# Dilated attention in a hybrid block: V as weights on column halves, unsplit fp32 scores, shares spread by TensorE, y_b products between the attention groups

## The chip, the core and the metric

The kernel runs on one core of one Trainium2 chip. TensorE multiplies, VectorE (DVE), ScalarE (ACT) and GpSimd (POOL) work on tiles, and SyncE (SP) issues most of the DMAs. The metric is device microseconds of one execution; less is better.

## The reference, cut to what matters

One decoder block on x of [1, 2048, 1024], all fp32. The part that the change touches:

```python
proj = x @ w_in + b_in            # q, k, v for 3 groups of 8 heads of 64, gates, RG-LRU input
q, k = rope(q), rope(k)
for g, (window, dilation) in enumerate(((128, 1), (512, 4), (2048, 16))):
    # per residue of the dilation, blocks of 128 queries against the block before and their own
    s = einsum(q, k) * 64 ** -0.5          # masked to a band
    m = max(s); p = exp(s - m); l = sum(p)
    o[g] = einsum(p, v) / l
    lse[g] = m + log(l)
attn = sum_g softmax_g(lse) * o[g]         # weighted over the three groups
y_a = (attn * silu(g_attn)) @ w_attn_proj
h = rg_lru(causal_conv(u))                 # the second branch
y_b = (h * silu(g_lru)) @ w_lru_proj
merged = sigmoid(gA) * y_a + sigmoid(gB) * y_b
x = layer_norm(ALPHA * x + merged @ w_out + b_out)
```

With dilation 16 a residue has 128 positions, one block, so there is no block before it.

## The kernel before

Large products run in fp32r: each fp32 operand is split into a high part and a rest, and three products (high by high, high by rest, rest by high) replace one. The order of work on every engine is that of the program text: the kernel schedules by hand, with `later(lag, fn)` putting a step off by some ticks and `run(late)` issuing what is due. All engines take their instructions in that order, each from its own queue.

There are four stages.

1. *Projection* (`product`, `evacuate`, the chains): x @ w_in in a seven-product block scheme, with rotary q and k stored to `qk_scr`, v to `v_scr`, gates to `ga_scr` and `mg_scr`, and the RG-LRU's result to `hb_scr`.
2. *Attention*, in 12 units (`unit(u)`): four pairs of heads `hp`, and for each the dilations 1, 16, 4 in this order. A unit has 16 query blocks of 128, taken in pairs `j` (96 in all).
   - `k_split` and `q_split` bring q and k of the next unit into high and rest, on ScalarE and GpSimd.
   - `scores(j)`: two blocks by two heads, three fp32r products each, into the PSUM tiles s0 and s1 (one per head, [128, 2, 256], two buffers each). The heads use the lower and upper 64 rows of TensorE.
   - `weigh(m)`: for each head VectorE adds the mask and takes the minimum of the negated scores (the negated maximum) in one operation (L1016); ScalarE takes the exponential (L1018). p is [query, key].
   - `turn_p(j)`: TensorE transposes p in 64-row halves into t0 and t1 (L1032); `copy_p(j, e)` copies them to SBUF, half on ScalarE (L1045), half mostly on VectorE (L1047).
   - `values(j)` (L1063): the turned p, 128x128, is the weight, and 65 columns of V move (64 and a column of ones, which gives the sum l), per block, head and key block. The result o is [query, head column] in a PSUM tile with two buffers. VectorE copies it to `osb` (L1068), and GpSimd's queue sends it with the minima to `o_scr`.
   - Two pairs j make a group of work on TensorE: transposes, scores, scores, transposes, values, values; values lag the scores by two to three pairs.
3. *y_b and combination*: 32 jobs `yb_job(n)`, n = (column chunk c, output tile f), of 24 matmuls of 128x512 (L1299 to L1301), each followed by VectorE's product with the gate. Between them run 16 `combine(c, hp)`: three `oc` tiles are loaded from `o_scr`, VectorE and ScalarE work out the shares of the three dilations, GpSimd weights and adds, TensorE turns the sum back to [head column, position] (L1235), VectorE multiplies by the gate, and the result goes to `at_scr`.
4. *y_a and output*: `ya_job` (L1374 to L1376) on tiles from `at_scr`, and `out_job` (L1411 to L1413), with the layer norm.

The y_b jobs start when the last value products have been issued, because their pools open there. PSUM has eight banks of 2 KB a partition; in the attention s0 and s1 take four, t0 and t1 two, o two.

The lines that a wait on o and s depends on:

```python
bank = [aps.tile([P, 2, 256], F32, tag=f"s{h}", name=f"s{h}{j}", bufs=2) for h in range(2)]
...
o = aps.tile([P, 2, 130], F32, tag="o", name=f"o{j}", bufs=2)
...
dve.tensor_copy(osb[:, b:b + 2, 0:130], o)
```

Of the kernel before, what the change touches and what calls it, by code (L numbers as in the profile page):

```python
# [15 lines left out]
P = 128  # L16
# [15 lines left out]
def hybrid_block_kernel(ctx: ExitStack, tc: tile.TileContext, a: dict, out: bass.AP):  # L32
# [10 lines left out]
    o_scr = [[dram.tile([S, 132], F32, name=f"o_scr{g}{hp}") for hp in range(HP)] for g in range(3)]  # L43
# [28 lines left out]
    bn = cst.tile([P, 72], F32, name="bn")  # L72
    lr = cst.tile([P, 8, 8], F32, name="lr")
# [23 lines left out]
    X = ctx.enter_context(tc.tile_pool(name="X", bufs=1))  # L97

    def big(slot, shape, dt, name):
        return (Y if slot[0] == "Y" else Z if slot[0] == "Z" else X).tile(shape, dt, name=name, tag=slot)  # L100

# [40 lines left out]
    LAST_SLOTS = [*range(15, 19), *range(29, 32), *range(28, 18, -1), *range(14, -1, -1)]  # L142
# [254 lines left out]
    def silu_chain(y, sgn, f, c):  # L397
# [3 lines left out]
        act.activation(y, y, AF.Identity, scale=0.5 * sgn, bias=bh[:, f:f + 1])  # L401
# [370 lines left out]
    QSLOT, KSLOT = ("X3", "X1", "Y0"), ("X4", "Y3")  # L772
    VSLOT = {(0, 0): "X5", (2, 0): "Y1", (1, 0): "Y2", (0, 1): "X5", (2, 1): "Y1", (1, 1): "Y2"}
    KR = {}

    units = {}
# [5 lines left out]
    def k_parts(u):  # L782

        g, hp = unit(u)
        src = qk_scr["k", 4 * g + hp].rearrange("(d h) s -> h d s", h=2)

        def part(h, hs):
            def fn():
                if h == 0 and u % 2 == 0:
                    KR["t"] = big(("X2", "X0")[u // 2 % 2], [P, 2, S], F32R, f"C{u}")  # L790
                if h == 0:
                    units[u] = [None, None, KR["t"][:, u % 2]]
                sp.dma_start(flat(units[u][2][hs]), src[h])
            return fn

        return [part(0, lo_), part(1, up_)]

    def k_split(u, x):

        if x == 0:  # L800
            units[u][1] = big(KSLOT[u % 2], [P, S], F32R, f"B{u}")

        def piece(t):
            if unit(u)[0] == 2:
                return t.rearrange("p (c x) -> p c x", c=4)[:, :, 256 * x:256 * x + 256]
            return t[:, 1024 * x:1024 * x + 1024]

        lo, hi = piece(units[u][2]), piece(units[u][1])
        pool.tensor_copy(hi, flat(lo))
        pool.tensor_tensor(out=lo, in0=flat(lo), in1=flat(hi), op=ALU.subtract)  # L810

    def q_parts(u):

        g, hp = unit(u)
        q = qk_scr["q", 4 * g + hp].rearrange("(d h) s -> h d s", h=2)

        def part(h):
            def fn():
                if h == 0:
                    units[u][0] = big(QSLOT[u % 3], [P, 2, S], F32R, f"A{u}")  # L820
                sp.dma_start(flat(units[u][0][(lo_, up_)[h], 1]), q[h])
            return fn

        return [part(h) for h in range(2)]

    def q_split(u, i):

        hi, lo = (units[u][0][:, x, i * CH:(i + 1) * CH] for x in range(2))
        act.activation(hi, flat(lo), AF.Copy)
        pool.tensor_tensor(out=lo, in0=flat(lo), in1=flat(hi), op=ALU.subtract)  # L830

    VT = {}

    def v_parts(g, j):
        src = v_scr[g][j]

        def part(i):
            def fn():
                if i == 0:
                    VT[g, j] = big(VSLOT[g, j], [P, 16, 260], F32, f"V{g}{j}")  # L840
                V = VT[g, j]
                if g == 0:
                    sp.dma_start(V[:, 4 * i:4 * i + 4], src[i * CH:(i + 1) * CH].rearrange("(n p) f -> p n f", p=P))
                elif g == 1:
                    sp.dma_start(V[:, 4 * i:4 * i + 4], src[i * CH:(i + 1) * CH].rearrange("(j r) f -> j r f", r=4))
                else:
                    sp.dma_start(V[:, 4 * i:4 * i + 4], src.rearrange("(i r) f -> i r f", r=16)[:, 4 * i:4 * i + 4])
            return fn

        return [part(i) for i in range(4)]  # L850


    def biases():
        dve.tensor_scalar(out=bh, in0=b72, scalar1=0.5, scalar2=None, op0=ALU.mult)
        dve.tensor_scalar(out=bn, in0=b72, scalar1=-1.0, scalar2=None, op0=ALU.mult)

# [45 lines left out]
    firstv = v_parts(0, 0)  # L902
    R0 = {}

    def first_raw(n):
        for i in K4:
            r = R0[n, i] = take(f"r{n}{i}", F32)
            src = qk_scr[n, 0].rearrange("(d h) s -> h d s", h=2)
            for h, hs in enumerate((lo_, up_)):
                sp.dma_start(r[hs], src[h][:, i * CH:(i + 1) * CH])  # L910

    def first_tiles():
        KR["t"] = big("X2", [P, 2, S], F32R, "C0")
        units[0] = [None, None, KR["t"][:, 0]]

    def first_split(n, i):
        if n == "q" and i == 0:
            units[0][0] = big(QSLOT[0], [P, 2, S], F32R, "A0")
        if n == "k" and i == 0:
            units[0][1] = big(KSLOT[0], [P, S], F32R, "B0")  # L920
        A, B, C = units[0]
        cs = slice(i * CH, (i + 1) * CH)
        hi, lo = (A[:, 0, cs], A[:, 1, cs]) if n == "q" else (B[:, cs], C[:, cs])
        r = R0[n, i]
        act.activation(hi, r, AF.Copy)
        tt(dve, lo, r, flat(hi), ALU.subtract)
        give(r)

    at(base[NQ - 2] + 2, lambda: first_raw("k"))
    at(base[NQ - 2] + 4, lambda: first_raw("q"))  # L930
    begin = {0: [first_tiles] + k_parts(1), 3: firstv, 5: q_parts(1)}
    split0 = {2: (("q", 0), ("q", 1)), 3: (("k", 0), ("k", 1)), 4: (("k", 2), ("k", 3)), 5: (("q", 2), ("q", 3))}
    low = NS
    where = [(s, j) for s in range(NQ) for j in range(ticks[s])]
    for T, (s, j) in enumerate(where):
# [10 lines left out]
        if s == NQ - 1:  # L946
            for fn in begin.get(j, ()):
                fn()
            for x in split0.get(j, ()):
                first_split(*x)  # L950
# [18 lines left out]

    stB = ctx.enter_context(ExitStack())  # L970
    at_p = stB.enter_context(tc.tile_pool(name="at_p", bufs=2, reuse_waits="tile"))
    Y = stB.enter_context(tc.tile_pool(name="Y", bufs=1, reuse_waits="tile"))
    aps = stB.enter_context(tc.tile_pool(name="aps", bufs=2, space=PSUM, reuse_waits="tile"))
    def prev(g, n):
        if g == 0:
            return n - 1 if n >= 1 else None
        if g == 1:
            return n - 4 if n >= 4 else None
        return None

    st = {}

    def scores(j):
        u, n0 = divmod(2 * j, 16)
        g, _ = unit(u)
        A, hi, low = units[u]
        bank = [aps.tile([P, 2, 256], F32, tag=f"s{h}", name=f"s{h}{j}", bufs=2) for h in range(2)]
        for b in range(2):
# [3 lines left out]
            for i, (x, B) in enumerate(((0, hi), (0, low), (1, hi))):  # L992
                for h, hs in enumerate((lo_, up_)):
                    if g == 2:
                        k = B[hs].rearrange("p (c r i) -> p r c i", c=4, r=16)[:, max(n - 1, 0):n + 1]
                    elif pv is None:
                        k = B[hs, n * P:(n + 1) * P]
                    elif g == 0:
                        k = B[hs, (n - 1) * P:(n + 1) * P]
                    else:  # L1000
                        c, r = divmod(n, 4)
                        k = B[hs, (c - 1) * CH:(c + 1) * CH].rearrange("p (c r j) -> p r c j", c=2, r=4)[:, r]
                    pe.matmul(bank[h][:, b, (0 if g == 2 and n else lo):256], A[hs, x, n * P:(n + 1) * P], k,  # L1003
                              start=(i == 0), stop=(i == 2))
            st["s", 2 * j + b] = (bank, lo)

    def weigh(m):
        n = m % 16
        bank, lo = st.pop(("s", m))
        if n % 4 == 0:  # L1010
            st["osb"] = at_p.tile([P, 4, 132], F32, tag="osb", name=f"osb{m}", bufs=6)
        osb = st["osb"]
        p = at_p.tile([P, 2, 256], F32, tag="p", name=f"p{m}", bufs=8)
        for h in range(2):
            mm = osb[:, n % 4, 130 + h:131 + h]
            dve.tensor_tensor_reduce(out=p[:, h, lo:256], in0=bank[h][:, m % 2, lo:256], in1=mask[:, lo:256],  # L1016
                                     scale=1.0, scalar=3e38, op0=ALU.add, op1=ALU.min, accum_out=mm)
            act.activation(p[:, h, lo:256], p[:, h, lo:256], AF.Exp, scale=-1.0, bias=mm)  # L1018
        st["p", m] = (p, lo, osb)

    def turn_p(j):
# [4 lines left out]
        for b in range(2):  # L1026
            p, lo, _ = st["p", 2 * j + b]
# [7 lines left out]
    def copy_p(j, e):  # L1035
        ptb, pt, los = st["t", j]
        on_act = e == 0 or j % 4 == 0
# [11 lines left out]
    def values(j):  # L1049
        u, n0 = divmod(2 * j, 16)  # L1050
        g, hp = unit(u)
        V = VT[g, hp // 2]
        vo = 130 * (hp % 2)
        ptb, _, los = st.pop(("t", j))
        o = aps.tile([P, 2, 130], F32, tag="o", name=f"o{j}", bufs=2)
        for b in range(2):
# [3 lines left out]
            for h in range(2):  # L1060
                for x in range(lo // P, 2):
                    kb = n if x else pv
                    pe.matmul(o[:, b, h * 65:h * 65 + 65], ptb[:, b, 2 * h + x, :],  # L1063
                              V[:, kb, vo + h * 65:vo + h * 65 + 65], start=(x == lo // P), stop=(x == 1))
        osb = st.pop(("p", 2 * j))[2]
        st.pop(("p", 2 * j + 1))
        b = n0 % 4
        dve.tensor_copy(osb[:, b:b + 2, 0:130], o)  # L1068
# [55 lines left out]
    for fn in v_parts(2, 0) + k_parts(2):  # L1124
        fn()
# [410 lines left out]
```

## Time and profile before

| what | us |
|---|---|
| median of 3 runs (2180.99 to 2183.07) | 2181.06 |
| the profiled execution, its own time | 2181.37 |
| its span, first to last instruction | 2179.5 |
| TensorE busy in the span | 2155.2 (99%) |
| VectorE busy | 1703.7 (78%) |
| ScalarE busy | 1220.3 (56%) |
| GpSimd busy | 774.1 (36%) |
| granted TensorE clock | 0.999 |

A busy TensorE isn't TensorE at its best: its records overlap, and a record's end is modelled. So the starts of neighbouring records, and periods of repeating work, say more than sums of durations. An engine is named with the line of the program that issued the instruction, `out<-in` by tile names, and an arrow after idle time names what ended it.

### The profile page before, as it was taken

How to read it: one execution, taken by the hardware profiler on the slowest of the kernel's cores; microseconds unless marked ns; L12 is line 12 of the kernel's file. 1: busy time of each engine (PE TensorE's matmuls, PEld its weight loads, DVE VectorE, ACT ScalarE, POOL GpSimd, SP SyncE). 2: the span in 40 equal slices, each digit the busy share in tenths (PEclk: the TensorE clock that was granted, in tenths of full speed). 3: DMA queues.
4: the chain of work that ended last, by engine and by line, in shares of the span. 5: the costliest groups of instructions: out<-in, count | busy, mean ns of one | idle time of the engine just before them, and what ended most of it. 6: DMA issues, size and time to landing. Idle time of an engine off the chain costs nothing.

```text
span 2179.5 us, 35322 instructions
## 1 busy us (share of the span) xinstructions
PE 2155.2 (99%) x12025; PEld 1803.7 (83%) x12025; DVE 1703.7 (78%) x3209; ACT 1220.3 (56%) x2206; POOL 774.1 (36%) x603
## 2 busy tenths in 40 slices
PE   9999999999999999999999999999999999999998
PEld 7888888888888888888888888879999878888786
DVE  8787987998899767687688798667777588867667
ACT  5456456557556666767767877758888511221100
POOL 2544554555555011021021021027666356622120
PEclk9999999999999999999999999999999999999999
DMA  7876976977877775676575675698774688864431
GB/s 227 255 220 195 264 228 204 265 224 235 256 216 230 242 221 172 184 220 175 184 221 165 198 230 176 189 292 242 208 196 130 191 282 281 263 203 149 156 116 68
DMA packets 257187, 456.05 MB, mean 209 GB/s; under 512 B 58752, under 2 KB 89504, under 8 KB 254192
## 3 DMA queue, kind: packets, MB, share of 16 engines
q1 hardware_dynamic: 237984, 412.70, 60.4%
q0 software_dynamic: 14128, 32.19, 7.1%
q10 hardware_dynamic: 4896, 8.92, 1.1%
q8 instruction: 95, 1.56, 0.3%
q14 instruction: 84, 0.69, 0.1%
HBM read 290.07 MB, written 163.64 MB: 208 GB/s over the span
## 4 chain that ended last, share of the span: by engine, by line
PE 55%; DMA 4%; issue 4%; DVE 2%; ACT 1%; POOL 1%; SPq 0%; ACTq 0%; POOLq 0%; DVEq 0%
PE q L627 32%; PE o L1063 5%; PE yb L1301 2%; PE yb L1299 2%; PE yb L1300 2%; PE s L1003 2%; PE pt L1032 2%; DMA V<-v_scr 1%; PE z L1413 1%; PE z L1412 1%; PE z L1411 1%; POOL me L1382 1%; PE g L488 1%; DMA atr<-at_scr 1%; ACT p L1018 1%
## 5 line engine op out<-in xcount | busy, mean ns | idle before, releaser
L627 PE MATMUL q<-xT,hS 128*128 128x512 f32 x1632 | 504.7, 390 | 0.0
L627 PE MATMUL q<-xT,l 128*128 128x512 f32 x1088 | 423.7, 389 | 0.1
L627 PE MATMUL q<-xB,hA 128*128 128x512 f32 x1344 | 417.4, 392 | 0.0
L627 PE MATMUL q<-xB,l 128*128 128x512 f32 x944 | 367.8, 390 | 1.7 <-DMA l<-wl_scr 1.7
L627 PEld LDWEIGHTS q<-xT,hS 128*128 128x128 f32 x1632 | 304.8, 188 | 64.3 <-issue 1.8
L627 PEld LDWEIGHTS q<-xB,hA 128*128 128x128 f32 x1344 | 250.4, 188 | 56.6 <-issue 5.5
L627 PEld LDWEIGHTS q<-xT,l 128*128 128x128 f32 x1088 | 204.2, 188 | 43.3 <-DMA l<-wl_scr 0.5
L233 POOL TENSOR_TENSOR sw<-sw,sin 128x512 f32<-128x512 f32 x96 | 155.8, 1628 | 167.8 <-ACT sw L322 71.3
L627 PEld LDWEIGHTS q<-xB,l 128*128 128x128 f32 x944 | 177.3, 188 | 39.4 <-DMA l<-wl_scr 2.1
L233 POOL TENSOR_TENSOR y<-y,h 128x512 f32<-128x512 f32 x28 | 39.2, 1399 | 384.1 <-DVE h L529 368.0
L627 PE MATMUL q<-xB,hS 128*128 128x512 f32 x544 | 168.8, 391 | 1.1 <-DVE v L233 1.1
L627 PE MATMUL q<-xT,hA 128*128 128x512 f32 x544 | 167.9, 390 | 0.0
L277 ACT ACTIVATE hA<-wA 128x512 fp32r<-128x512 f32 x220 | 138.6, 636 | 31.8 <-DVE l L233 11.6
L1018 ACT ACTIVATE p<-p,osb 128x256 f32<-128x256 f32 (+1 forms) x384 | 145.3, 451 | 18.9 <-DVE osb L1016 18.3
L277 ACT ACTIVATE hS<-S 128x512 fp32r<-128x512 f32 x170 | 108.4, 638 | 64.4 <-DVE S L233 46.1
L1063 PE MATMUL o<-V,ptb 128*128 128x65 f32 x1200 | 144.4, 277 | 0.0
L1063 PEld LDWEIGHTS o<-V,ptb 128*128 128x128 f32 x1200 | 137.7, 192 | 3.3
L233 POOL TENSOR_TENSOR l<-wA,hA 128x512 fp32r<-128x512 f32 x68 | 110.3, 1622 | 84.7 <-ACT hA L277 51.2
L1016 DVE CUSTOM_DVE_ANT_0 p<-s,mask 128x256 f32<-128x256 f32 (+1 forms) x384 | 116.9, 361 | 24.2 <-PE s L1003 16.9
L627 PEld LDWEIGHTS q<-xB,hS 128*128 128x128 f32 x544 | 101.2, 188 | 22.6 <-issue 2.2
L627 PEld LDWEIGHTS q<-xT,hA 128*128 128x128 f32 x544 | 101.8, 188 | 21.8 <-ACT hA L277 0.4
L233 DVE TENSOR_TENSOR S<-S,wA 128x512 f32<-128x512 f32 x102 | 98.2, 963 | 11.6 <-DMA wA<-in_w_in_dram 8.1
(207 smaller groups left out, 4645.8 us busy)
## 6 DMA issues: line engine op xcount, KB each, us to landing
wA<-in_w_in_dram SPq DMA_DIRECT2D x220, 256.0 KB, 5.1
wl_scr<-l SPq DMA_DIRECT2D x102, 512.0 KB, 5.3
l<-wl_scr SPq DMA_DIRECT2D x102, 512.0 KB, 4.4
wS<-in_w_in_dram SPq DMA_DIRECT2D x102, 256.0 KB, 4.3
wS<-in_w_in_dram POOLq DMA_DIRECT2D x68, 256.0 KB, 6.9
mg_scr<-y SPq DMA_DIRECT2D x59, 256.0 KB, 5.1
o_scr<-osb POOLq DMA_DIRECT2D x48, 264.0 KB, 5.4
oc<-o_scr SPq DMA_DIRECT2D x48, 264.0 KB, 4.9
```

The source lines that it names most:

```text
L233: eng.tensor_tensor(out=out, in0=in0, in1=in1, op=op)
L277: act.activation(heads(h), heads(r, False), AF.Copy)
L488: pe.matmul(g, gw[hs, l], x[hs], start=(n == 0), stop=(n == 2))
L627: pe.matmul(bank, w[:, ks], x[:, kk, xx], start=(first and i == 0), stop=(last and i == 11))
L1003: pe.matmul(bank[h][:, b, (0 if g == 2 and n else lo):256], A[hs, x, n * P:(n + 1) * P], k, start=(i == 0), stop=(i == 2))
L1016: dve.tensor_tensor_reduce(out=p[:, h, lo:256], in0=bank[h][:, m % 2, lo:256], in1=mask[:, lo:256], scale=1.0, scalar=3e38, op0=ALU.add, o ...
L1018: act.activation(p[:, h, lo:256], p[:, h, lo:256], AF.Exp, scale=-1.0, bias=mm)
L1032: pe.transpose(pt[e][:, b, 2 * h + x, :], p[hs, h, x * P:(x + 1) * P], ident[hs, hs])
L1063: pe.matmul(o[:, b, h * 65:h * 65 + 65], ptb[:, b, 2 * h + x, :], V[:, kb, vo + h * 65:vo + h * 65 + 65], start=(x == lo // P), stop=(x == 1))
L1299: pe.matmul(yb, WL[f][:, 0, k], xx[:, 0], start=(k == 0), stop=False)
L1300: pe.matmul(yb, WL[f][:, 0, k], xx[:, 1], start=False, stop=False)
L1301: pe.matmul(yb, WL[f][:, 1, k], xx[:, 0], start=False, stop=(k == 7))
```

## The change

- Scores are one fp32 product in place of three fp32r ones; the splits of q and k are gone, and q, k are loaded into two buffers of their own. For dilation 16 the product has 128 columns, not 256.
- `values(j)`: V is the weight, 64 columns per head without the column of ones, and the turned p moves (128 columns), in fp32 as before. The two heads write the lower and upper 64 partitions of one PSUM tile. The result is [head column, query] already. All pairs share one tile `OB` of [128, 2, 2, 128]; pair j uses `OB[:, j % 2]`. VectorE copies it, with a stride for dilations 4 and 16, into tiles that stay in SBUF (`o_tile(u)`); `o_scr` is gone.
- The sum l comes from the exponential's accumulator. Minima and sums of a unit lie in a tile `ML`, which `turn_ml` transposes and sends to `ml_scr`.
- The shares of a pair of heads are worked out at once on 32 partitions (`load_ml`, 28 small loads; `weights`, with four steps; 8 stores to `w_scr`). `spread` brings them to all partitions with a matmul by a 0/1 matrix `sel` (fp32r, 128x512), VectorE multiplies, GpSimd adds and multiplies by the gate. 48 spreads replace 16 combines.
- The attention is written in 48 groups G of two pairs. From G = 4 on each group ends with half a y_b product (12 matmuls): 44 halves, 22 products. The other 20 halves follow the attention. y_b has one PSUM bank inside (`s` four, `t` two, `OB` one) and four after it.
- Weights and h for y_b are split by GpSimd inside; the factor 0.5 on w moved to the gate's activation (`bq`).

The diff, cut:

```diff
 def scores(j):
-    A, hi, low = units[u]
+    q, k_ = AT_X["qk", u % 2][:, 0], AT_X["qk", u % 2][:, 1]
     bank = [aps.tile([P, 2, 256], F32, tag=f"s{h}", name=f"s{h}{j}", bufs=2) for h in range(2)]
...
-            for i, (x, B) in enumerate(((0, hi), (0, low), (1, hi))):
-                for h, hs in enumerate((lo_, up_)):
...
-                    pe.matmul(bank[h][:, b, (0 if g == 2 and n else lo):256], A[hs, x, n * P:(n + 1) * P], k,
-                              start=(i == 0), stop=(i == 2))
+            for h, hs in enumerate((lo_, up_)):
...
+                pe.matmul(bank[h][:, b, lo:256], q[hs, n * P:(n + 1) * P], k, start=True, stop=True)
 def weigh(m):
...
-            act.activation(p[:, h, lo:256], p[:, h, lo:256], AF.Exp, scale=-1.0, bias=mm)
+            act.activation(p[:, h, lo:256], p[:, h, lo:256], AF.Exp, scale=-1.0, bias=mm, accum_out=ll)
 def copy_p(j, e):
-        on_act = e == 0 or j % 4 == 0
+        on_act = e == 0
 def values(j):
-        o = aps.tile([P, 2, 130], F32, tag="o", name=f"o{j}", bufs=2)
+        o = OB[:, j % 2]
         for b in range(2):
...
-                    pe.matmul(o[:, b, h * 65:h * 65 + 65], ptb[:, b, 2 * h + x, :],
-                              V[:, kb, vo + h * 65:vo + h * 65 + 65], start=(x == lo // P), stop=(x == 1))
+                for h, hs in enumerate((lo_, up_)):
+                    pe.matmul(o[hs, b, :], V[:, kb, 64 * h:64 * h + 64], ptb[:, b, 2 * h + x, :],
+                              start=(x == lo // P), stop=(x == 1))
...
-        dve.tensor_copy(osb[:, b:b + 2, 0:130], o)
+        dst = o_tile(u)
...
+        dve.tensor_copy(dst, o)
+    OB = aps.tile([P, 2, 2, P], F32, name="ob", bufs=1)
+    def spread(hp, c, g, tag):
+        cs = slice(c * CH, (c + 1) * CH)
+        os = [o_tile(3 * hp + UG[x])[:, cs] for x in range(3)]
+        w = cur["ps"].tile([P, CH], F32, tag=tag, name=f"w{hp}{c}{g}", bufs=cur["wb"])
+        pe.matmul(w, sel[:, g], st["wh", hp, c], start=True, stop=True)
+        tt(dve, os[g], os[g], w, ALU.mult)
...
+    for G in range(NG + 1):
+        run(late)
+        if G < NG:
+            if G:
+                turn_p(2 * G - 2)
+                copy_p(2 * G - 2, 0)
+                copy_p(2 * G - 2, 1)
+            scores(2 * G)
+            weigh(4 * G)
+            weigh(4 * G + 1)
+            scores(2 * G + 1)
+            if G:
+                turn_p(2 * G - 1)
+                copy_p(2 * G - 1, 0)
+                copy_p(2 * G - 1, 1)
+            weigh(4 * G + 2)
+            weigh(4 * G + 3)
+            for j in (2 * G - 3, 2 * G - 2):
+                if j >= 0:
+                    values(j)
...
+        for fn in todo.pop(G, ()):
+            fn()
+        y = G >= GY and (G < NG or len(halves) % 2)
+        if y:
+            n, hf = divmod(halves[0], 2)
+            yb_part(n, 4 * hf)
+            yb_part(n, 4 * hf + 1)
+        for i, x in enumerate(spreads.pop(G, ())):
+            spread(*x, f"t{i}")
+        if G % 4 == 0 and G:
+            turn_ml(G // 4 - 1)
+        if y:
+            yb_part(n, 4 * hf + 2)
+            yb_part(n, 4 * hf + 3)
+            if hf:
+                yb_done(n)
+            yb_care(halves.pop(0))
```

`todo` holds the loads and the steps of the shares by group: for a pair of heads whose last unit ends with group e − 1 the 28 loads are issued in group e + 1, VectorE's first step follows in e + 2, and its 12 spreads stand in the groups e + 6 to e + 11, two in each. `yb_done` is VectorE's product with the gate, `yb_care` loads and splits what the next halves need. The last pair's shares are worked out beside the 20 halves after the attention.

More of the change, by code (lines that the diff above doesn't have):

```diff
@@ L900, in hybrid_block_kernel @@
             at(max(t, 0), fn)
[L902 to L908, printed above, removed]
[L909 to L932 removed]
+    begin = {1: qk_parts(0), 3: v_parts(0)}
     low = NS
@@ L1452, in hybrid_block_kernel @@
     split_m(TT[0], slice(6, 8))
-    run(late)
-    assert not late
+    while late:
+        run(late)
+        now["n"] += 1
     load_xr(TT[0])
```

640 lines of the change are left out of this document (336 added, 304 removed).

## The prediction, before the change was run

> **What bounds the kernel now.** I read the stretches first, cut where the attention starts (1456.0), where its last value product ends (1720.1) and where the first y_a product starts (1904.8).
>
> ```profile
> core 0: us, PE busy (x) PEld busy (x) DVE busy (x) ACT busy (x) POOL busy (x), PEclk, DMA share, GB/s
> 0.00:1456.00 1456.00, 1449.92 (x6491) 1187.55 (x6491) 1178.05 (x1578) 929.92 (x1509) 459.42 (x347) 1.00 0.72 217
> 1456.00:1720.10 264.10, 260.12 (x3554) 250.28 (x3553) 193.45 (x941) 221.90 (x572) 169.11 (x145) 1.00 0.71 198
> 1720.10:1904.80 184.70, 182.69 (x835) 150.12 (x834) 143.89 (x376) 33.63 (x71) 99.00 (x81) 1.00 0.84 268
> 1904.80:2179.50 274.70, 262.48 (x1155) 215.78 (x1152) 188.26 (x316) 34.87 (x54) 46.52 (x30) 0.99 0.41 138
> ```
>
> The change touches the two middle stretches, 264.1 + 184.7 = 448.8 us. TensorE is busy in 98% of both, so its order of work sets the time. Next the chain of waits, for one period of four query blocks: first with a previous key block (dilations 1 and 4), then without (dilation 16).
>
> ```profile
> 1511.51 0.64 PE pt L1032 x16
> 1512.14 1.48 PE s L1003 x24
> 1513.63 0.49 PE pt L1032 x16
> 1514.12 3.72 PE o L1063 x32
> 1517.84 0.64 PE pt L1032 x15
> 1518.48 1.47 PE s L1003 x22
> ...
> 1557.88 0.39 PE pt L1032 x8
> 1558.27 1.50 PE s L1003 x21
> 1559.77 0.24 PE pt L1032 x8
> 1560.02 1.93 PE o L1063 x16
> 1561.95 0.39 PE pt L1032 x8
> 1562.34 1.34 PE s L1003 x23
> ```
>
> The periods are 6.34 us (1512.14 to 1518.48) and 4.07 us (1558.27 to 1562.34). Only TensorE stands in them: transposes, scores, transposes, values. The values (L1063) are the dearest part. Now VectorE in the same periods:
>
> ```profile
> 1513.04 0.42 DVE L1016 CUSTOM_DVE_ANT_0 p<-s,mask 128x256 f32<-128x256 f32 x1 [1.07 <-PE s L1003]
> ...
> 1514.43 0.69 DVE L1047 COPY ptb<-pt 128x512 f32<-128x512 f32 x1
> 1515.03 0.41 DVE L1016 CUSTOM_DVE_ANT_0 p<-s,mask 128x256 f32<-128x256 f32 x1
> ...
> 1516.40 0.42 DVE L1068 COPY osb<-o 128x260 f32<-128x260 f32 x1
> ...
> 1559.18 0.29 DVE L1016 CUSTOM_DVE_ANT_0 p<-s,mask 128x128 f32<-128x128 f32 x1 [0.84 <-ACT ptb L1045]
> ...
> 1561.32 0.42 DVE L1068 COPY osb<-o 128x260 f32<-128x260 f32 x1
> ```
>
> Its queue is: four mask operations, one copy of turned p, four more, and only then the first copy of o. From the first mask operation to the end of that copy are 1516.82 − 1513.04 = 3.78 us with a previous block and 1561.74 − 1559.18 = 2.56 us without. Today no one waits for this copy, because o has two PSUM buffers.
>
> One more reading, on how finely a wait on PSUM is drawn:
>
> ```profile
> 1511.95 0.36 PE L1003 MATMUL s<-B,A 64*128 64x256 f32 x2
> 1512.15 0.28 PE L1003 MATMUL s<-C,A 64*128 64x256 f32 x2
> 1512.27 0.40 PE L1003 MATMUL s<-B,A 64*128 64x256 f32 x4
> 1512.52 0.28 PE L1003 MATMUL s<-C,A 64*128 64x256 f32 x2
> 1512.63 0.40 PE L1003 MATMUL s<-B,A 64*128 64x256 f32 x4
> ```
>
> Twelve products belong to one pair of blocks, six to each block, and a head's two blocks lie side by side in one PSUM tile of 2 KB a partition. The first block's six have ended at about 1512.55. VectorE, idle for 1.07 us, starts on it at 1513.04, 0.12 after the twelfth (1512.64 + 0.28). So it waited for writes to the other half of the tile: the wait covers the tile, not the half that is read.
>
> **The change part by part.** Its prices start from these rows:
>
> ```profile
> L1063 PE MATMUL o<-V,ptb 128*128 128x65 f32 x1200 | 144.4, 277 | 0.0
> 1768.57 0.62 PE ctp L1235 x4
> ```
>
> *Scores, fp32 unsplit.* Today 24 fp32r records of 256 columns take 1.47 us, two heads side by side: 0.1225 per pair. An fp32 product is two records: L1063 has 1200 records for 600 products. No row shows an fp32 record of 256 columns. Lower end: as fast as fp32r, 0.1225 per pair. Upper end: the o record, 3.72/32 = 0.116 for 65 columns, scaled to 256 gives 0.46. That row reloads a full 128x128 of weights each time, so part of it is not columns; I take twice the fp32r rate, 0.226 a pair, nearer the lower end. A block pair with previous keys then costs 4 x 0.226 = 0.90, without 4 x 0.12 = 0.48: four blocks 1.81 and 0.96 against 1.48. No gain on TensorE. It does free ScalarE and GpSimd of the splits, which nobody waits for.
>
> *Values.* Today 32 records take 3.72 us per four blocks. After, V is the weight (64 columns), 128 columns move, and the two heads use column halves. Half of the 256-column price, 0.118 per pair of records, gives 16 pairs = 1.88 (no previous block 0.94): 1.84 less. If the halves don't run beside each other it is 3.76. That they do is inferred from the row halves of the scores; no run here shows column halves.
>
> *Transposes* stay: 0.64 + 0.49 to 0.64.
>
> *y_b.* A half product is 12 matmuls. From the second stretch, (184.70 − 16 x 0.62)/768 = 0.228 each, 2.73 a half. 44 halves move inside. It is the same work, and lengthens each group.
>
> *The copy of o.* Here I see the decision. o is now one tile OB of [128, 2, 2, 128] fp32, 2 KB a partition, and pairs of blocks use its halves in turn. In each group TensorE does values(2G−3), then values(2G−2) into the other half. If the wait covers the tile, as for s above, values(2G−2) must wait for VectorE's copy of 2G−3, which is queued behind all eight mask operations and a copy of turned p. Behind the waiting matmul queue the y_b half and all of the next group. Worked out from the start of the first scores, with previous blocks: scores 0.90, VectorE starts 0.165 later (as 1512.14 + 0.735 against 1513.04), its queue 3.78, restart 0.15 (estimate, from the 0.12 to 0.165 between engines above), values 0.94, y_b 2.73, transposes 0.64: 9.31. TensorE's own work is 0.64 + 1.81 + 0.64 + 1.88 + 2.73 = 7.70, so it idles about 1.6. Without previous blocks: 0.48 + 0.165 + 2.56 + 0.15 + 0.47 + 2.73 + 0.39 = 6.94 against 5.41. Today's price of the same work is 6.34 + 2.73 = 9.07 and 4.07 + 2.73 = 6.80.
>
> The Trainium skill, "PSUM — Partial Sum Buffer", section "PSUM bank collisions raise a hardware error", says software must order any two engines that touch one bank in the same quadrant of partitions, even at different addresses; by that rule the halves of OB exclude each other, and the s rows agree (0.49 us waited past the first block's products).
>
> For dilations 4 and 16 the copy now writes with a stride. The nearest rows:
>
> ```profile
> L233 DVE TENSOR_TENSOR rp<-y,sw 128x512 f32<-128x512 f32 x64 | 90.7, 1417 | 2.6 <-POOL sw L233 1.9 <-DVE y L326 0.2
> L233 DVE TENSOR_TENSOR y<-y,sw 128x512 f32<-128x512 f32 x32 | 29.8, 933 | 0.2
> ```
>
> A strided write is 1.5 times as long there: 0 to 0.2 per copy, 0 to 7 us in 32 groups. I take 0.
>
> *Shares.* Removed: 16 combines with 0.62 on TensorE each (9.9) and the o_scr traffic. Added: 48 spreads of 0.228 (36 inside, 8.2; 12 later, 2.7), 12 small transposes at about 0.3 (3.3 inside). Per head pair 28 small loads go through SP:
>
> ```profile
> L843 SPq DMA_DIRECT2D V<-v_scr x8: 377/504/994, 1447.9 to 1554.5; - x8
> ```
>
> At 0.38 to 0.50 each that is 11 to 14 us, more than the group of 9.3 between the loads and VectorE's first operation on them; a late load blocks VectorE in order, hence its mask operations. 0 to 6 per head pair; I take 3, 12 in all. Also queued behind those loads are wl and gB, which have a group or two to spare.
>
> *Start.* The splits of the first unit go; q, k (2 MB) come from the last step's second product on, some 16 us ahead. Taken at nothing; if they are late it costs the wait. Ramp and drain of the attention, 8 (estimate: about one group without y_b).
>
> *Sum.* With a previous block are 28 of 48 groups (all 16 of dilation 1, 12 of 16 of dilation 4), without 20. 28 x 9.31 + 20 x 6.94 = 399.5; less four first groups without y_b, 10.9; plus 8.2 + 3.3 + 8: 408.1. After it 20 halves, 54.6, and 2.7. With 12 for the shares, 477.4 against 448.8: +28.6. The stretches ahead and behind stay. The profiled execution took 2181.4 (span 2179.5 and 1.9 around it), 0.3 above the median of 2181.06. So 2210.
>
> Ends for the unknown prices, the wait standing: only the first scores and the second values of a group are on the path. fp32 at its lower end gives 0.41 + 0.30 less per group with previous blocks (values bounded by 0.08 for a pair of transposes), half without: −27, 2183. Column halves one after the other: 28 x 0.94 + 20 x 0.47 = +36, 2246. The upper fp32 price in scores as well, 28 x 0.93 + 20 x 0.47 more, would give about 2281.
>
> The Trainium skill, "TensorEngine Tiling (Array Packing)", section "Key Properties", says a change of the tiling mode drains TensorE, and the change adds a mode. The rows show transposes in row halves followed by o in the full array with no visible gap (1513.63 + 0.49 = 1514.12); by the rule at some 0.16 a switch it would be 8 us more, 2218.
>
> **The rivals.**
> 1. *The halves of OB don't wait on each other* (other side). Then TensorE stays full: 28 x 7.70 + 20 x 5.41 = 323.8 in place of 399.5, 2134. For it: only a read after writes is seen to cover the tile, no write after a read. Against: the same tile and engines. It decides from the point where the wait is under about 1.0 us a group (28.6/48 = 0.6 of the 1.6).
> 2. *Column halves run one after the other*: 2246. For it: no row shows them. Against: row halves do run together (0.1225 for two).
> 3. *fp32 runs at the lower prices with the wait standing*: 2183, no change to speak of. Against: the o record at 0.116 for 65 columns.
> 4. *The loads of the maxima hold up VectorE*, at 6 to 9 for each of four head pairs: 24 more than taken at most, 2234. For it: SP's 11 to 14 us. Against: the group is nearly as long.
>
> **How the numbers follow.** Forecast 0.47, rival 1 0.25, rival 2 0.10, rival 3 0.12, rival 4 0.06. A measurement of this kernel can tell about 0.2%, 4 us. Faster: nearly all of rival 1, a third of rival 3 and a little of the forecast's edge, 0.30. Same: half of rival 3 and a little of the forecast, 0.08. Slower 0.62. The forecast's own range is 2190 to 2232 (strides +7, drains +8, shares −12 to +12, ramp). With rivals 1 and 2 taken in, the whole range is 2130 to 2246.
>
> **What would show it.** In the changed trace: periods of about 9.3 and 6.9 between first scores in groups with y_b; TensorE's values row idle before itself, released by VectorE's copy, some 1.5 us for each of 48; TensorE busy near 83% in the attention. If that idle is missing, and periods are 7.7 and 5.4, rival 1 holds. Four records of 256 fp32 columns for two heads in 0.45, and four of 128 columns in 0.24, would bear out the prices; 0.47 for the latter is rival 2. VectorE idle before the first minimum over groups, released by a DMA, is rival 4. The forecast is wrong if something fills the wait, or if q and k come late at the start.

## The result, and the profile after

The changed kernel takes 2280.47 us (median, 2276.66 to 2283.97) against 2181.86 beside it: 1.0451 of the time before, 95% interval 1.0432 to 1.047. It is slower, as forecast, but by 99 us and not by 29; 2280 lies outside the range. The profiled execution took 2283.97 us (span 2282.2).

The stretches of the changed kernel, cut as before: first scores (1452.5), last value product (1908.3), first y_a product (2007.1).

```profile
core 0: us, PE busy (x) PEld busy (x) DVE busy (x) ACT busy (x) POOL busy (x), PEclk, DMA share, GB/s
1452.50:1908.30 455.80, 361.02 (x3745) 285.25 (x3744) 256.68 (x1031) 232.74 (x899) 191.25 (x228) 0.94 0.62 162
1908.30:2007.10 98.80, 67.41 (x255) 49.55 (x254) 48.61 (x59) 25.19 (x44) 38.52 (x35) 0.86 0.53 167
2007.10:2282.20 275.10, 262.60 (x1153) 215.65 (x1151) 190.87 (x318) 37.99 (x59) 45.93 (x30) 0.99 0.42 141
```

The middle stretches, 448.8 us before, are now 455.8 + 98.8 = 554.6; the forecast had 477.4. The rest stayed (3.5 less ahead, 0.4 more behind). TensorE, busy 99% of both before, is at 79% and 68%, and its granted clock, 1.00 before, is 0.94 and 0.86. Its groups, with the idle time before each and what ended it:

```profile
L1188 PE MATMUL yb<-hx,wl 128*128 128x512 f32 x256 | 114.5, 447 | 28.1 <-ACT hx L1170 14.4 <-ACT wl L1155 13.1 <-DVE o L1042 0.5
L1032 PE MATMUL ob<-ptb,V 128*64 128x128 f32 x1200 | 93.7, 296 | 70.0 <-DVE o L1042 69.9
L1002 PE MATMUL pt<-ident,pt 64*128 64x64 f32 x1200 | 58.2, 230 | 22.7 <-ACT ptb L1015 22.2 <-ACT pt L988 0.4
```

The 70.0 us at the values were forecast. The 22.2 at the transposes and the 28.1 at y_b were not. One undisturbed group, on TensorE and then on VectorE:

```profile
1686.63 1.95 PE L974 MATMUL s<-qk 64*128 64x256 f32 x16
1688.41 0.66 PE L1002 MATMUL pt<-ident,pt 64*128 64x64 f32 x16
1689.00 1.09 PE L1032 MATMUL ob<-ptb,V 128*64 128x128 f32 x16
1691.65 1.09 PE L1032 MATMUL ob<-ptb,V 128*64 128x128 f32 x16 [1.55 <-DVE o L1042]
1695.62 0.59 PE L1002 MATMUL pt<-ident,pt 64*128 64x64 f32 x12
```

```profile
1687.75 0.42 DVE L986 CUSTOM_DVE_ANT_0 pt<-s,mask 128x256 f32<-128x256 f32 x1
...
1690.83 0.42 DVE L986 CUSTOM_DVE_ANT_0 pt<-s,mask 128x256 f32<-128x256 f32 x1
...
1691.18 0.42 DVE L1042 COPY o<-ob 128x256 f32<-128x256 f32 x1
```

This is the forecast's picture: the second values start 0.05 us after VectorE's copy of the first half of OB ends (1691.60), and that copy stood behind eight masks and a copy of turned p. Such groups take 9.5 us (9.52 from first score to first score; 9.31 forecast), and 7.03 without a previous block (6.94 forecast). (7.03 holds where that copy still writes without a stride; with one the next group takes 7.23.) What failed lies in the other groups and behind the attention. Three causes can be read off.

**The clock.** A group where the wait is longer. Its first values belong to blocks without a previous one and end sooner (0.66 us in place of 1.09), while its scores and masks are already full width; the copy of o, with a stride, takes 0.58 us at 1516.57 in place of 0.42:

```profile
1514.48 0.66 PE L1032 MATMUL ob<-ptb,V 128*64 128x128 f32 x8
1517.21 0.66 PE L1032 MATMUL ob<-ptb,V 128*64 128x128 f32 x8 [2.07 <-DVE o L1042]
1517.80 0.50 PE L1188 MATMUL yb<-hx,wl 128*128 128x512 f32 x1
1518.13 0.39 PE L1189 MATMUL yb<-hx,wl 128*128 128x512 f32 x1
...
1519.15 0.63 PE L1189 MATMUL yb<-hx,wl 128*128 128x512 f32 x1
1519.58 0.63 PE L1190 MATMUL yb<-hx,wl 128*128 128x512 f32 x1
```

After this wait of 2.07 us the y_b products go from one each 0.23 us to one each 0.43, and the group takes 10.5 us. But the length of the wait does not settle it: the clock also fell after a wait of 1.74 us that ended at 1548.88, and stayed at 1.00 after another of 2.07 that ended at 1642.67. Three pairs of stretches, each the 3.41 us ahead and the 3.41 us that follow, for these three waits:

```profile
1515.02:1518.43 3.41, 1.34 (x15) 0.96 (x12) 2.65 (x11) 3.24 (x14) 0.00 (x0) 1.00 1.00 197
1518.43:1521.84 3.41, 3.41 (x10) 2.63 (x9) 0.10 (x1) 0.00 (x0) 0.00 (x0) 0.50 1.13 317
1545.74:1549.15 3.41, 1.67 (x34) 1.36 (x30) 2.95 (x14) 3.41 (x14) 0.00 (x0) 1.00 0.82 189
1549.15:1552.56 3.41, 3.41 (x21) 2.70 (x18) 0.61 (x1) 0.40 (x2) 0.00 (x0) 0.50 0.56 123
1641.31:1644.72 3.41, 2.05 (x14) 1.65 (x15) 1.92 (x8) 2.41 (x11) 0.00 (x0) 1.00 1.05 203
1644.72:1648.13 3.41, 3.41 (x33) 2.68 (x33) 2.60 (x4) 0.60 (x1) 1.38 (x2) 1.00 1.10 345
```

The cuts follow the trace. Every change of the granted clock behind 1452 lies a whole number of 3.41 us from every other, and it is 1.00 or 0.50 in between. Ahead of each of the 13 falls up to 2007, TensorE was busy in at most 0.49 of such a stretch of 3.41 us; a stretch at full clock with 0.50 or more was never followed by a fall. So a wait costs clock where enough of it falls into one stretch.

**The change of h's chunk.** Around 1590 to 1640, what ScalarE waited for, and TensorE:

```profile
ACT hx L1170 <- DMA hx<-hb_scr: 10.2, 4, 7.2
ACT hx L1170 <- PE w L1121: 4.2, 1, 4.2
```

```profile
PE pt L1002 <- ACT ptb L1015: 8.3, 2, 5.9
```

`split_h` stands on ScalarE one group after its loads were issued, the loads have not landed, and the copies of turned p queue behind it. (The list of the change says that GpSimd splits h inside. That holds for the first chunk; from the second on ScalarE makes the high part, L1170, 16 times in the attention.) The groups 19, 20, 35 and 36 take 16.8, 12.7, 16.8 and 17.0 us.

**The part behind the attention.** SyncE, with the first and last lines of the last head pair's 28 loads and the loads behind them, and TensorE's waits there:

```profile
1909.49 0.48 SPq L1058 DMA_DIRECT2D mt<-ml_scr  x1
1912.87 0.73 SPq L1060 DMA_DIRECT2D mt<-ml_scr  x1
...
1925.77 0.82 SPq L1064 DMA_DIRECT2D mt<-ml_scr  x2
1926.64 0.83 SPq L1144 DMA_DIRECT2D wlr<-in_w_f_dram  x2
...
1928.98 2.17 SPq L1163 DMA_DIRECT2D hx<-hb_scr  x4
```

```profile
PE yb L1188 <- ACT hx L1170: 14.4, 1, 14.4
PE yb L1188 <- ACT wl L1155: 13.1, 3, 7.2
```

The 28 loads hold SyncE from 1909.5 to 1926.6, and the loads that the y_b halves need stand behind them.

### The profile page after: what moved, and what is told of

Same layout as the page of the kernel before. It is cut to its first block, busy times and chain, and to the rows that moved or that the text cites. A ratio compares the mean times of both kernels' runs of the same rounds, so it can differ in the third digit from the quotient of the medians.

```text
span 2282.2 us, 34836 instructions
## 1 busy us (share of the span) xinstructions
PE 2139.0 (94%) x11637; PEld 1737.8 (76%) x11637; DVE 1671.9 (73%) x2980; ACT 1222.4 (54%) x2504; POOL 735.0 (32%) x641
## 5 line engine op out<-in xcount | busy, mean ns | idle before, releaser
L988 ACT ACTIVATE pt<-pt,ml 128x256 f32<-128x256 f32 (+1 forms) x384 | 171.8, 449 | 22.9 <-DVE ml L986 22.8
L1032 PE MATMUL ob<-ptb,V 128*64 128x128 f32 x1200 | 93.7, 296 | 70.0 <-DVE o L1042 69.9
L280 ACT ACTIVATE hA<-wA 128x512 fp32r<-128x512 f32 x220 | 138.5, 635 | 29.9 <-DVE l L236 11.4
L1188 PE MATMUL yb<-hx,wl 128*128 128x512 f32 x256 | 114.5, 447 | 28.1 <-ACT hx L1170 14.4
L1032 PEld LDWEIGHTS ob<-ptb,V 128*64 128x64 f32 x1200 | 68.8, 145 | 85.4 <-DVE o L1042 81.0
L986 DVE CUSTOM_DVE_ANT_0 pt<-s,mask 128x256 f32<-128x256 f32 (+1 forms) x384 | 116.9, 361 | 5.5 <-PE s L974 3.6
```

Of the source, the lines that this page charges most:

```text
L280: act.activation(heads(h), heads(r, False), AF.Copy)
L1032: pe.matmul(o[hs, b, :], V[:, kb, 64 * h:64 * h + 64], ptb[:, b, 2 * h + x, :], start=(x == lo // P), stop=(x == 1))
L1188: pe.matmul(YB["t"], w[:, 0, k], x[:, 0], start=(k == 0), stop=False)
```

## The experiments

Times are medians; ratios are to the kernel before on the same chip, with their 95% interval.

**Is it the copy of o?** e1 moves the first values of a group, and with them their copy, up by one step of the order:

```
             scores(2 * G + 1)
+            if 2 * G - 3 >= 0:
+                values(2 * G - 3)
             if G:
                 turn_p(2 * G - 1)
...
-            for j in (2 * G - 3, 2 * G - 2):
-                if j >= 0:
-                    values(j)
+            if G:
+                values(2 * G - 2)
```

> Edit: in each group values(2G-3) and its copy go ahead of the second transposes and the last four mask operations; nothing else moves, OB stays one tile. Theory (the wait on the one OB tile, queued behind VectorE's masks, costs 70 us of idle TensorE and most of the clock's drops in the attention): the idle before L1032 falls from 70 to under 10 us, groups with a previous block go from 9.5 to about 7.9, without from 7.0 to about 5.7, the attention from 455.8 to 370 to 390, the total to 2200 to 2215. Rival (VectorE's or ScalarE's queue is the limit, and the idle only shows at values): the idle moves to the transposes, the total stays above 2260.

Measured 2224.44 us, ratio 1.0199 (1.0178 to 1.0219): 56 less than the changed kernel, somewhat short of the 65 to 80 expected. The wait went as expected, in the groups by line:

```profile
L1032 PE MATMUL ob<-ptb,V 128*64 128x128 f32 x1200 | 91.5, 291 | 6.7 <-DVE o L1042 5.0
L1002 PE MATMUL pt<-ident,pt 64*128 64x64 f32 x1200 | 60.4, 236 | 24.3 <-ACT ptb L1015 23.7 <-ACT pt L988 0.4
```

70.0 to 6.7 at the values; the 22 at the transposes stayed, so that is another cause.

**Is it the shared tile?** e3 and e4 leave the attention without y_b (`GY = 49`, all 64 halves come behind it); e4 gives OB two tiles, a tile being free there without y_b:

```
-    OB = aps.tile([P, 2, 2, P], F32, name="ob", bufs=1)
+    OB = [aps.tile([P, 2, P], F32, name=f"ob{i}", bufs=1) for i in range(2)]
...
-        o = OB[:, j % 2]
+        o = OB[j % 2]
```

> Edit: no half y_b product stands inside the attention; all 64 halves follow it; OB one tile. This gives the attention part alone. Theory: groups of 9.5 - 2.7 = 6.7 with and 7.0 - 2.7 = 4.6 without a previous block (the latter ScalarE's: 8 x (0.29 + 0.19) + 0.74), the attention 275 to 290 against 264 before the change, then 64 x 2.73 + 3 = 178 and up to 10 for the shares: total 2190 to 2205. Rival (new scores and values are dear in themselves, and a slow clock adds to it): attention above 310, total above 2230.

> Edit: as the run without y_b inside, and OB is two tiles in two PSUM banks. Theory: the idle before the values, released by VectorE's copy, is gone (under 5 us); but without y_b ScalarE is then the next limit: 8 x (0.40 + 0.19) + 2 x 0.58 = 5.9 a group with and 4.6 without a previous block, so the attention falls by only 15 to 25 us against the run with one tile, total 2170 to 2185. Rival (the wait was never the tile's): no difference within 5 us, and the same idle.

Measured 2351.38 (ratio 1.0772, 1.0754 to 1.0791) and 2304.10 (1.0559, 1.0544 to 1.0575). The values' row of e3, then that of e4:

```profile
L1032 PE MATMUL ob<-ptb,V 128*64 128x128 f32 x1200 | 101.7, 314 | 65.5 <-DVE o L1042 65.4
```

```profile
L1032 PE MATMUL ob<-ptb,V 128*64 128x128 f32 x1200 | 83.9, 294 | 0.0
```

With a tile for each half the wait is 0.0, with nothing moved: it is the shared tile, not VectorE's load. Part of the time shows up elsewhere: the idle time before the transposes goes from 38.7 us to 71.0 (40.4 of it ended by ScalarE's copy), and the attention falls by 49.0 us, not by 65. The Trainium skill, "PSUM — Partial Sum Buffer", section "PSUM bank collisions raise a hardware error", has the rule by which software must order two engines in one bank; these two rows agree with it. They do not tell the tile from its bank, since e4 parts both. The times are far off what was expected: both are over 100 us too slow, and e3 lies where its rival put it (attention above 310, total above 2230). The attention in e3 and in e4, and e3's y_b part:

```profile
1450.00:1836.50 386.50, 268.99 (x3218) 215.58 (x3216) 241.75 (x1010) 223.47 (x883) 90.45 (x124) 0.81 0.51 121
1836.50:2079.00 242.50, 202.59 (x781) 155.88 (x782) 89.14 (x125) 64.33 (x107) 60.56 (x51) 0.88 0.58 185
```

```profile
1451.00:1788.50 337.50, 234.43 (x3218) 194.74 (x3217) 232.94 (x1009) 220.32 (x883) 90.50 (x124) 0.87 0.59 138
```

And the scores of one of e3's groups:

```profile
1636.36 2.71 PE L974 MATMUL s<-qk 64*128 64x256 f32 x16
1638.91 0.66 PE L1002 MATMUL pt<-ident,pt 64*128 64x64 f32 x16
```

Without y_b in its groups TensorE is 70% busy and its clock 0.81 and 0.87; the scores of one of its groups take 2.55 us and not 1.78. At full clock they cost what was forecast, so the rival's first reason (dear in themselves) falls and its second, the clock, stands. Besides, TensorE now waits 38.7 us at the transposes and 11.7 at the spreads. With y_b in the groups the clock was 0.94: y_b inside the attention earns more than its place. And the y_b part takes 3.8 us a half where the kernel before took 2.9, 17.3 and 15.6 us of it waits for the splits of wl and h.

**The chunk change.** e2 issues `split_h` two groups after the loads (`later(1, ...)` becomes `later(2, ...)`).

> Edit: split_h of the next chunk comes two ticks after its loads, not one. Theory (ScalarE stands in order before a load of h that has not landed, and holds up its copies of turned p, so four groups at the two chunk changes inside take 12.7 to 17.0 us in place of 7 to 9.5, and in the tail TensorE waits 14.4 us once): those four groups fall by about 28 us in sum, the tail by about 10, the total to 2240 to 2250. Rival (the loads are late because SP is blocked, so one tick more does not reach them): less than 10 us in all, above 2270.

Measured 2251.48, ratio 1.0329 (1.0301 to 1.0356), 29 less, just outside the 2240 to 2250 expected; the row of the transposes:

```profile
L1002 PE MATMUL pt<-ident,pt 64*128 64x64 f32 x1200 | 57.2, 227 | 6.0 <-ACT ptb L1015 5.5 <-ACT pt L988 0.4
```

The attention fell from 455.8 to 427.1 us, the 28 expected: TensorE's idle time by 13.3 (this wait by 16.7; the one for the copy of o grew by 2.5), its busy time by 15.4 for the same 3745 products, with the clock at 0.98 in place of 0.94. The part behind the attention fell by 3.3 us and not by 10, and the wait of 14.4 us there stayed (14.7).

**Filling the wait in place of removing it.** e8 leaves the copy where it is and puts the first six y_b products between the two values:

```
-            for j in (2 * G - 3, 2 * G - 2):
-                if j >= 0:
-                    values(j)
+            if 2 * G - 3 >= 0:
+                values(2 * G - 3)
+            if G >= GY:
+                n, hf = divmod(halves[0], 2)
+                yb_part(n, 4 * hf)
+                yb_part(n, 4 * hf + 1)
+            if G:
+                values(2 * G - 2)
...
-        if y:
-            n, hf = divmod(halves[0], 2)
-            yb_part(n, 4 * hf)
-            yb_part(n, 4 * hf + 1)
```

> The changed kernel with one edit: the first six y_b products of a group stand between values(2G-3) and values(2G-2) and not behind both. The copy of o stays where it is in VectorE's queue and the bank stays one. Theory: the wait is the time that the copy needs, whatever TensorE does in it, so 1.4 us of work of its own covers most of the 1.5 us of each group: idle at the values falls from 70.0 us to 10 to 25, the mean clock in the attention goes up from 0.94 with it, and the time is 2225 us (2210 to 2245). Rival: VectorE is what sets the group's length, the wait moves to the transposes behind it, and the time is 2265 us or more.

Measured 2238.76, ratio 1.0262 (1.0247 to 1.0278), inside the theory's bounds. Idle at the values is 9.7 us, but the clock rose only to 0.95: the waits at the chunk change are still there.

**Both repairs, and then the part behind the attention.** e5 has the edits of e1 and e2. e6 issues the last pair's loads of its first two units at groups 45 and 46, so that 8 of 28 are left behind the attention. e7 also stores the last shares two halves later, with what follows, and takes the subtraction of h's last chunk to VectorE:

```
+    at_group(45, lambda: load_ml(3, (0,)))
+    at_group(46, lambda: load_ml(3, (1,)))
...
-            7: [lambda: step(3, 4)], 8: [lambda: load_wh(3, 3), lambda: load_wh(3, 0)],
+            9: [lambda: step(3, 4)], 10: [lambda: load_wh(3, 3), lambda: load_wh(3, 0)],
...
-        pool.tensor_tensor(out=t[:, 1], in0=flat(t[:, 1]), in1=flat(t[:, 0]), op=ALU.subtract)
+        (pool if i < 24 else dve).tensor_tensor(out=t[:, 1], in0=flat(t[:, 1]), in1=flat(t[:, 0]), op=ALU.subtract)
```

> The two edits of e1_early and e2_h_later together. Theory: they take away different idle time (the values' wait for VectorE's copy, 70.0 us in the changed kernel and 6.7 in e1_early; the transposes' wait for ScalarE's copy of the transposes behind the split of h, 22.2 us and 5.5 in e2_h_later), so their gains add: 2280 - 56 - 29 = 2195 us (2185 to 2205), ratio to the kernel before 1.002 to 1.011, and both waits are small in the one trace. Rival: once the attention is shorter the loads of h come later against it and the second gain is gone: 2215 us or more.

> As e5_early_h_later, and of the last head pair's 28 loads of minima and sums on SyncE, the 4 and 16 that belong to its first two units are issued at groups 45 and 46, inside the attention, so that 8 are left behind it. Theory: the 13.7 us of SyncE's queue ahead of the loads of wl, gB and h in the y_b part behind the attention is one of two holds there; it shrinks to some 4 us, and that part goes from 97 us to some 87: 2185 us (2175 to 2193). Rival: the other hold, the store of the shares that stands on SyncE until GpSimd has made them (15.4 us of wait in e2_h_later), takes its place, and the time is that of e5_early_h_later within 4 us.

> As e6_tail_loads, and the store of the last shares two y_b halves later (with the loads and products that follow it), and the subtraction in the split of h's last chunk on VectorE in place of GpSimd, so that the shares don't queue behind it. Theory: what is left of the y_b part behind the attention is then its own 20 halves at 2.9 us and 12 spread products, some 65 to 70 us in place of 97: 2165 us (2153 to 2180), faster than the kernel before. Rival: the chain minima, shares, spread, stored product, y_a is as long as the part itself, the wait only moves to y_a, and the time is 2180 us or more.

Measured 2208.85 (ratio 1.013, 1.0115 to 1.0145), 2203.55 (1.0105, 1.0088 to 1.0122) and 2187.43 (1.0033, 1.0012 to 1.0054). The gains of e1 and e2 add to 72 of 85 us, which is 4 us outside the theory's range and short of its rival's 2215. The part behind the attention in e5, e6 and e7:

```profile
1838.20:1934.60 96.40, 70.22 (x254) 52.72 (x255) 52.05 (x59) 25.73 (x44) 38.31 (x35) 0.82 0.53 174
```

```profile
1834.60:1925.00 90.40, 71.67 (x254) 51.98 (x255) 51.95 (x59) 25.77 (x44) 37.24 (x35) 0.87 0.58 184
```

```profile
1833.00:1906.70 73.70, 63.36 (x254) 49.22 (x254) 51.20 (x67) 26.22 (x44) 28.60 (x27) 0.95 0.66 218
```

The 20 loads that were taken out give 6 us, the store and the split together 17 more (they were not run apart): the second hold, SyncE standing at the store until GpSimd had made the shares (15.4 us in e6, 4.8 in e7), was the larger one, nearer to the rival of e6 than to its theory. At 2187 e7 missed the theory's 2165 and lies where its rival put it, but not for the rival's reason: y_a waits only 0.6 us. The part behind the attention came within 4 us of the 65 to 70 expected; of the 22 us missed, 14 were missing in e5 already (2209 for 2195). Inside the attention the groups 15, 27 and 39 take 13.2 to 13.4 us in e7 (11.4, 10.5 and 11.7 in the changed kernel): with shorter groups the loads of a pair's minima land later against them. ScalarE around group 15 of e7:

```profile
ACT mt L1093 <- POOL mt L236: 6.6, 1, 6.6
```

**The shares inside the attention.** e9 has the shares' exponentials one group later (`(1, 2, 2, 3, 4)` becomes `(1, 2, 3, 3, 4)`); e10 also spreads the loads of every pair:

```
+    for hp in range(4):
+        e = 12 * hp + 12
+        at_group(e - 3, lambda hp=hp: load_ml(hp, (0,)))
+        at_group(e - 2, lambda hp=hp: load_ml(hp, (1,), (0, 1)))
+        at_group(e - 1, lambda hp=hp: load_ml(hp, (1,), (2, 3)))
```

> As e7_tail_all, and the exponentials of the shares (the step that ScalarE takes part in) one group later for the three head pairs inside the attention. In e7_tail_all the groups 15, 27 and 39 take 13.2 to 13.4 us in place of 8.05, ScalarE standing 6.6 us in one of them at the shares' exponentials (they wait for GpSimd, that for VectorE's minima, those for the last of the 28 loads) with its copies of the transposes queued behind. Theory: one group later the loads have landed, ScalarE doesn't stand, and each of the three groups comes down by some 4 to 5 us, part of it kept because VectorE still stands at the minima (1.8 and 3.8 us): 2187 - 9 = 2178 us (2172 to 2183). Rival: VectorE's stand alone holds the group, and the time stays within 3 us of 2187.

> As e9_sums_later, and for every head pair the 4 and 16 loads of its first two units go out in the three groups before its last unit ends, so that 8 and not 28 follow it. Theory: the minima find their loads landed, neither VectorE nor ScalarE stands, the groups 15, 27 and 39 take 8 to 9 us, and the first spread of a pair no longer waits for its shares (5.2 us at the spreads in e7_tail_all): 2187 - 15 - 3 = 2169 us (2163 to 2177), faster than the kernel before by some 0.5%. Rival: the loads only move, and hold up the loads of q, k, V and w_f1 on SyncE in the groups before; then no better than e9_sums_later.

e9: ratio 1.0036 (1.0023 to 1.0049), no gain on e7. ScalarE no longer stands, VectorE does: the rival was right (4.7 us at the transposes, now released by VectorE's copy). e10: 2184.66, ratio 1.0002 (0.9989 to 1.0015). The groups 15, 27 and 39 fell to 8.1, as expected, but 16, 28 and 40 rose from 7.1 to 9.3, 9.2 and 10.8 (VectorE's reciprocal waits 3.4 us for GpSimd's sums there), so some 7 us of gain came, by the two ratios, where 18 were expected.

**The last two waits.** e11 moves the loads and splits of wa three halves later (`2 + i` becomes `5 + i`) and the second unit's q and k ahead of the second four loads of h.

> As e10_all_pairs, with two moves: the loads and splits of wa in the y_b part behind the attention three halves later (ScalarE stands there 4.1 us for a war load, with the split of h's last chunk queued behind it, and TensorE 6.9 us for that split), and the loads of the second unit's q and k ahead of the second four loads of h in group 1 (the wait of 1.8 us at the scores of group 4, which takes 10.9 us in place of 6.5). Theory: both waits go to near 0 and the clock stays up around them: 2184 - 4 - 4 = 2176 us (2171 to 2182), a little faster than the kernel before. Rival: h's own load, issued behind 5.6 us of loads of minima and sums on SyncE, is late as well, and q and k are late for another reason: within 3 us of 2184.

Measured 2181.21, ratio 0.9995 (0.9984 to 1.0007). Group 4 fell from 10.9 to 7.3; TensorE's longest wait for the split of h only from 6.9 to 5.2, as the rival says of it. The time fits both the theory's range and the rival's, and against e10 the intervals overlap, so no gain is shown. Attention and part behind it in e11:

```profile
1452.00:1822.10 370.10, 347.17 (x3745) 267.41 (x3744) 255.76 (x1031) 236.79 (x899) 191.57 (x228) 1.00 0.76 200
1822.10:1899.60 77.50, 67.23 (x254) 50.45 (x254) 52.43 (x67) 26.14 (x44) 28.54 (x27) 0.89 0.63 204
```

370.1 + 77.5 = 447.6 us against 448.8 before. So in this order the new way of computing costs what the old one did: the 99 us were the order of the work around it, which e1 to e11 change while the products stay. No version here beats the kernel before by more than can be measured.

## Why the prediction was wrong in size

*The copy of o: right.* Place, releaser and price came out as written, 9.52 and 7.03 us a group for 9.31 and 6.94; idle 70.0 us at the values, for about 1.5 in each of 48. e1 and e4 show the cause from two sides.

*The prices of fp32: near, the first by luck.* Scores of four blocks took 1.78 us (1688.41 − 1686.63) for 1.81. But 0.226 a pair was called twice the fp32r rate, and twice 0.1225 is 0.245, which gives 1.96; that the slip lies beside the measured 0.22 is chance. Values of a pair with previous blocks are 0.94 by the prediction and took 1.02, start to next start; without, 0.59 for 0.47. Rivals 2 and 3 fall: the two heads' records start 0.007 us apart and the next two 0.11 us later (changed kernel, 1691.81 to 1692.14), so column halves do run beside each other, and fp32 is not as fast as fp32r. No run shows the 0.16 us a switch by which the prediction priced a change of the tiling mode.

*The chunk change: the step that failed.* The prediction lists the y_b work as "the same work" that "lengthens each group" and does not follow `split_h`, which moved with it, through ScalarE's queue. It cost 29 us (e2), as idle time and as slow clock.

*The shares: mis-sized.* 3 us for each of four pairs, 12 in all, and "wl and gB, which have a group or two to spare". For the three pairs inside the attention that was about right, if anything high: VectorE stood 8.8 us at the loads in all three, and the groups 15, 27 and 39 are longer by 5.0 in sum. For the last pair it was not: behind the attention a half lasts 2.7 us and not 9, so the spare time is gone, and 98.8 us stand where the sum had 54.6 + 2.7 + 3 = 60.3. e7 won back 23 of the 38, most of it by the store and the split, which the prediction has not at all. Rival 4 named the right loads, but the wrong victims and the wrong place.

*The clock: not a term at all.* The rows of before had 1.00 in both stretches, and the prediction took that over. With TensorE waiting it was 0.94 and 0.86. Of the 455.8 us of the attention 54.6 passed at half clock, 34.1 of them at the two changes of h's chunk and 20.5 after waits for the copy of o.

*Strides: taken at 0 out of 0 to 7.* A group is longer by 0.2 us where its first copy writes with a stride (7.23 for 7.03), so some 6 us in 32 groups, an estimate from these two periods.

*Rival 1 was priced too low.* With the wait nearly gone and the clock at 1.00, e11's attention takes 370 us; the rival's full TensorE would take 408.1 − (399.5 − 323.8) = 332, with the shares 341. Undisturbed groups take 8.0 and 6.2 to 6.7 us where it has 7.70 and 5.41. A little of that shows where the kind of product changes: in e11 the first y_b product after values is followed at 0.33 us, the others at 0.23. Removing the wait alone (e1), the other waits standing, gave 2224 us, not 2134.

The miss adds up: attention 455.8 for 408.1 + 9 (38.7, of which e2 shows 28.7), the part behind it 98.8 for 60.3 (38.5), 3.1 less elsewhere: 74 us on 2210, which is the 2284 of the profiled execution, 3.5 above the median. No run takes the other 10 us of the attention apart; the strides and the 20.5 us at half clock after the copy's waits stand there. Behind the attention 13.4 us over the sum are left in e7, of which TensorE is idle 10.3.

## What to carry to other kernels

When work is moved beside other work, follow each of its loads and splits into the queue that it now stands in, and ask who is behind it; spare time counted in groups shrinks with the group. Price a wait on TensorE twice, once as idle time and once as the slower clock that can follow it (here where TensorE was busy in less than about half of 3.41 us). Double buffering is only that if the two halves don't share a PSUM tile; where no second one is to be had, moving the producer ahead of the queue in front of the copy (e1) does better than filling the gap (e8).

## What the hardware showed that was not expected

Waits shorter than 3.41 us, the step on which the clock changed, were enough to halve it: it fell after 1.74 us and after 2.07, and after others as long it did not. What sorts them is TensorE's busy share in the 3.41 us ahead, with the border near a half. In the changed kernel falls follow shares up to 0.49, and the lowest share that kept the clock is 0.47. Over the traces of the changed kernel and of all eleven runs, from 1450 to 2100 us, falls follow shares up to 0.60, and no share under 0.47 kept the clock. The Trainium skill, "TensorE: Matmul & The Clock Gate", section "Why this matters for your kernels", asks for no idle gaps over some 3 us; by the rows above that is not strict enough here. The same page of the Trainium skill, section "A second HAM failure mode: psum-queue depth-cycling", tells of short idle times between groups that make the clock swing, and with that the trace agrees: 13 falls and as many returns from 1452 to 2007.

That an attention at 70% of TensorE without y_b ran at a clock of 0.81, and the same with y_b at 0.94, makes filler work worth more than its own time. Counting transposes as idle time does not sort the stretches of the changed kernel: two with a share of 0.32 kept the clock and one with 0.42 lost it, so the transposes seem to count as work. That is read from traces; no run varies it. A second tile for OB with y_b inside was not tried.
